# Latent attention of a hybrid backbone: two places for a pair's keys, three or four for its queries, keys split from PSUM, queries copied whole and rotated in SBUF

## The chip, the cores and the metric

One core of one Trainium2 chip runs the whole program in one launch. The metric is the device time of one execution in microseconds (us). A time is the median of several runs of the same program; one further execution was taken by the hardware profiler, and all rows shown here come from that one.

## The reference, cut to what matters

Two layers run over 256 latent tokens (the x stream) and 256 context tokens. Each layer mixes tokens in three ways (A windowed grouped-query attention, B multi-head latent attention, C gated linear attention), merges the three branches by gates, and ends with a gated convolutional feed-forward network. The second layer has no context output. The change touches branch B alone:

```
q  = (rmsnorm(cq)  @ w_uq ).reshape(.., 8 heads, 64 + 32)   # 64 plain, 32 rotary columns a head
kv = (rmsnorm(ckv) @ w_ukv).reshape(.., 8 heads, 64 + 64)   # 64 key columns, 64 value columns a head
q_rot = rope(q[.., 64:])        # latent tokens only; context queries stay as they are
k_rot = rope(bkr)               # one rotary key of 32 columns, shared by all 8 heads
s = (q_plain . k_plain + q_rot . k_rot) * 96 ** -0.5
out = softmax(s) @ v            # latent queries read context and latent keys, context queries context keys
```

## The kernel before, in words

Tokens lie along the free axis: a tile of 128 partitions and 512 columns holds 128 features of 256 latent and 256 context tokens. In layer 0 a query tile has W = 512 columns (NS = 2 streams), in layer 1 only the 256 latent ones (NS = 1). Every fp32 product is made of three matmuls on pieces of reduced precision: `mm3` multiplies hi by hi, hi by lo and lo by hi. A tile is cut into these pieces by `split(src, hi, lo)`: ScalarE (ACT) casts src to hi, VectorE (DVE) writes src - hi to lo. In the trace these are lines L188 and L189; for weights they are L164 (ACT) and L168 (DVE or GpSimd, POOL), both in `load_w`.

`attn_run` runs branch A and then branch B, each over four pairs of heads, with the score steps (pair, stream, half of the queries): 16 steps a branch in layer 0, 8 in layer 1. In a step, `scores` issues the matmuls of L818 into the PSUM tile `s`, takes the row maximum (L824), the exponentials (L834) and scales them (L840). `step_on` then does one part of what the next pair needs, and `values` of the step before transposes its probabilities (L856) and splits them (`pth` on L860, `ptl` on L861). Between the steps stand the fills: units of the merge of another branch (a gate of eight k-tiles or a product of four), which keep TensorE (PE) busy; L783, L787 and L789 read their PSUM. `outputs` (L872, L875) multiplies the probabilities with the values once both halves of a stream are there.

For branch B the next pair's parts are, from `prep_b(pr)`, in this order: `keys`, `vals`, `queries(0)`, `queries(1)`; then `ready()` is called behind the scores of the pair's last step and hands over the operands of the next pair's scores. In layer 0 one part goes with each of four steps, in layer 1 all go within two.

- `keys` multiplies into a PSUM tile `kp` and copies its two halves of 64 rows to SBUF (`kf`, L936).
- `queries(hh)` multiplies into a PSUM tile `qp`, whose rows are 64 plain columns, 32 rotary ones, and the same 32 again with the halves exchanged. ACT copies rows 0 to 63 to `qf` (L945), DVE forms the rotary rows with two products that read `qp` (L947, L948) and a sum (L949), and in layer 0 ACT copies the context half of the rotary rows (L951).
- `ready()` splits `kf` and `qf` of both heads. There is one place for a pair's keys, the tiles `kh` and `kl` (L420 to L424), which branch A's keys had before; the rotary rows 64 to 95 of it are split from `cgk` once, for the first pair. The queries have two places, the tag `q` (L426).

`kp`, `qp`, the values' tile and the fills all take turns on the PSUM tag `mm`, which has two banks. Each engine executes its queue in order. The order in the queues is laid down when the program is built: a planner goes through the instructions by their place in the source and by when it takes them to be ready.

Of the kernel before, what the change touches and what calls it, by code (L numbers as in the profile page):

```python
# [7 lines left out]
F32R = mybir.dt.float32r  # L8
# [3 lines left out]
ALU = mybir.AluOpType  # L12
# [6 lines left out]
T = 256  # L19
NTOK = 512  # L20
# [12 lines left out]
def hybrid(nc, tc, I, out, dbg=None, stop=None):  # L33
# [3 lines left out]
    V, S, G = nc.vector, nc.scalar, nc.gpsimd  # L37
# [5 lines left out]
    def pool(name, bufs=1):  # L43
        return tc.tile_pool(name=name, bufs=bufs, reuse_waits="tile")
# [5 lines left out]
    def psum(tag, w=512):  # L50
        return ps.tile([128, 512], F32, tag=tag, name="ps_" + tag, bufs=2)[:, :w]
# [11 lines left out]
    def wtile(name):  # L63
        return small.tile([128, 512], F32, tag="w", name=name, bufs=4)
# [4 lines left out]
    tabB = cst[:, C_TB:C_TB + 256]  # L69
# [101 lines left out]
    def mm3(o, ah, al, bh, bl, start, stop):  # L171
        mm(o, ah, bh, start=start, stop=False)  # L172
        mm(o, ah, bl, start=False, stop=False)  # L173
        mm(o, al, bh, start=False, stop=stop)  # L174
# [12 lines left out]
    def split(src, hi, lo, eng=None):  # L187
        S.copy(hi, src)  # L188
        (eng or V).tensor_tensor(out=lo, in0=src, in1=hi.bitcast(F32), op=ALU.subtract)  # L189
# [127 lines left out]
    def layer(l):  # L317
        last = l == L - 1
        lo_on_pool(0, 1)
        W = T if last else NTOK  # L320
        NS = W // T
# [3 lines left out]
        def inunit(t, w, p=None):  # L325
            return unit(win[l, t], Hh, Hl, w, p=p)
# [7 lines left out]
        with pool(f"mods{l}") as mp:  # L334
            if not last:
# [11 lines left out]
                                       in1=cs.rearrange("p (k s) -> p k s", s=2), op0=ALU.add, op1=ALU.mult)  # L347
# [32 lines left out]
            for streams in ([[0], [1]] if last else [[0, 1]]):  # L380
                c0, wd = T * streams[0], T * len(streams)
                for k in range(KT):
                    q = slice(c0, c0 + wd)
# [33 lines left out]
        cgk = yb_.tile([96, NTOK], F32, name="cgk")  # L417
        av_ = yb_.tile([128, 4, 2, 2, 64], F32R, name="av")

        def k_tile(n):  # L420
            return yb_.tile([128, 2, NTOK], F32R, tag="kh", name="kh")[:n]

        def l_tile(n):
            return yb_.tile([128, 2, NTOK], F32R, tag="kl", name="kl")[:n]  # L424

        def q_tile(n):  # L426
            return yb_.tile([128, 2, W], F32R, tag="q", name="q", bufs=2)[:n]
# [6 lines left out]
        with pool(f"c{l}") as cp:  # L434
# [17 lines left out]
            t1 = small.tile([128, 256], F32, tag="r1", name="t1", bufs=1)  # L452
# [87 lines left out]
            for t in range(2):  # L540
                gg = pair2("st"[t])
                for d in range(2):
                    g = gg[:, d]
# [10 lines left out]
            for t in range(2):  # L554
                for d in range(2):
                    g = mn[t][:, d]
# [93 lines left out]
            def rope_raw(t, w, scale):  # L650
                raw = wtile("araw")
                S.activation(raw[:, :w], inunit(t, w), AF.Copy, scale=scale)
                return raw
# [4 lines left out]
            for t in range(2):  # L658
                kx = cp.tile([128, 2 * NTOK], F32, tag="ex", name="kx", bufs=3).rearrange("p (a b) -> p a b", a=2)[:, :, :T]
# [9 lines left out]
            for t in range(2):  # L669
                kx = kxs[t]  # L670
# [65 lines left out]
            def rope(raw, bank="mm"):  # L736
                rp = psum(bank, T)
                mm(rp, perm, raw[:, :T], start=True, stop=True)
                t1 = small.tile([128, 256], F32, tag="r1", name="t1", bufs=1)
                V.tensor_tensor(out=t1, in0=rp, in1=sinA, op=ALU.mult)  # L740
                G.tensor_tensor(out=raw[:, :T], in0=raw[:, :T], in1=cosA, op=ALU.mult)
                V.tensor_tensor(out=raw[:, :T], in0=raw[:, :T], in1=t1, op=ALU.add)
# [56 lines left out]
        common = st2.enter_context(pool(f"att{l}"))  # L799
# [119 lines left out]
                    pv()  # L919
            return hd.get(4)  # L920

        kb, yb = [], []

        def prep_b(pr):
            if pr == 4:
                return [], None
            vb = common.tile([128, 4, 2, 2, 64], F32R, tag="vb", name="vb", bufs=2)
            kf, qfs, kv = [], [], []

            def keys():  # L930
                kv.extend(load_w(I["wukv"][l, pr], 256))
                kp = psum("mm")
                mm3(kp, kv[0][:, :128], kv[1][:, :128], ckh, ckl, True, True)
                for i in range(2):
                    kf.append(wtile("kf")[0:64])
                    S.copy(kf[i], kp[64 * i:64 * i + 64])  # L936

            def queries(hh):
                uqh, uql = load_w(I["wuq"][l, pr][:, 256 * hh:256 * hh + 256], 256)
                qp = psum("mm", W)  # L940
                for k in range(2):
                    c = slice(128 * k, 128 * k + 128)
                    mm3(qp, uqh[:, c], uql[:, c], cqh[k], cql[k], k == 0, k == 1)
                qf = wtile("qf")[:96, :W]
                S.copy(qf[0:64], qp[0:64])  # L945
                t1 = small.tile([128, 256], F32, tag="r1", name="t1", bufs=1)
                V.tensor_tensor(out=t1[64:96], in0=qp[64:96, :T], in1=tabB[64:96], op=ALU.mult)  # L947
                V.tensor_tensor(out=qf[64:96, :T], in0=qp[96:128, :T], in1=tabB[96:128], op=ALU.mult)  # L948
                V.tensor_tensor(out=qf[64:96, :T], in0=qf[64:96, :T], in1=t1[64:96], op=ALU.add)  # L949
                if NS == 2:  # L950
                    S.copy(qf[64:96, T:], qp[64:96, T:])  # L951
                qfs.append(qf)

            def vals():
                p = psum("mm")
                for tt in range(4):
                    c = slice(128 * tt, 128 * tt + 128)
                    mm3(p[:, c], ckh[:, c], ckl[:, c], kv[0][:, 128:256], kv[1][:, 128:256], True, True)
                split(p.rearrange("p (a h d) -> p a h d", a=4, h=2), vb[:, :, :, 0], vb[:, :, :, 1])

            def ready():
                if pr == 0:
                    kb.extend([k_tile(96), l_tile(96)])
                    for i in range(2):
                        split(cgk[64:96], kb[0][64:96, i], kb[1][64:96, i])
                qq = []
                for i in range(2):
                    split(kf[i], kb[0][0:64, i], kb[1][0:64, i])
                    qb = q_tile(96)
                    qh, ql = qb[:, 0], qb[:, 1]  # L970
                    split(qfs[i], qh, ql)
                    qq.append([(qh, kb[0][:, i]), (qh, kb[1][:, i]), (ql, kb[0][:, i])])
                return qq, vb, lambda: (yb[0][pr], yb[1][pr])
            return [keys, vals, lambda: queries(0), lambda: queries(1)], ready

        def prep_a(j):
            if j == 4:
                return prep_b(0)
            q, qt = [], [] if j else [q2]
            parts = [] if j == 0 else [lambda: q.append(rope_raw(T_AQ + j, W, 0.125)), lambda: rope(q[0])]  # L980

            def ready():
                if j:
                    qt.append(q_tile(128))
                    q_halves(q[0], qt[0])
                return [[(qt[0][:, i], k2[:, i]), (qt[0][R[i], i], kl[R[i]])] for i in range(2)], av_, lambda: (yah(j), yal[j])
            return parts, ready
# [58 lines left out]
        with pool(f"f{l}") as fp, ExitStack() as rst:  # L1046
# [3 lines left out]
            for s in range(NS):  # L1050
                q = slice(T * s, T * s + T)
# [244 lines left out]
```

## Time and profile before

| what | value |
|---|---|
| median of 3 runs | 1510.85 us (1507.99 to 1511.19) |
| the profiled execution | 1507.28 us, of which the span from the first to the last instruction is 1505.1 us |
| PE, share of the span in matmuls | 95% |
| DVE busy | 81% |
| ACT busy | 54% |
| POOL busy | 31% |
| granted TensorE clock, mean | 0.99 |
| branch B's score steps | about 330 to 446 us (layer 0) and 1155 to 1240 us (layer 1) |

A row of the timeline gives the start in us, the duration, the engine, the line, the operation, what it writes and reads, and in brackets how long its engine was idle before it and what ended that. A row of waits gives who waited for whom, the total in us, the number of times and the longest. A matmul row lasts longer than it holds the engine: matmuls overlap, and their ends are modelled, so the time that PE loses is read from its idle time.

### The profile page before, as it was taken

To read this page: it belongs to the slowest core of one execution; us is meant where nothing else is said; L and a number is where in the kernel's file an instruction comes from. 1 tells how busy PE (TensorE), PEld (TensorE's weight loads), DVE (VectorE), ACT (ScalarE), POOL (GpSimd) and SP (SyncE) were. 2 spreads that over 40 slices of the span, in tenths; PEclk is the share of its full clock that TensorE was granted. 3 is DMA by queue.
4 is the path that set the end of the run, shared out by engine and by line. 5 is a ranking of instruction groups with operands and counts; after the bars stand their busy time and mean duration, and the time that the engine had idled before them with its cause. 6 is when DMAs were issued, how large, how long until landed. Compare 5 with 4: busy or idle time off the path is not lost. (4 is left out here: it accounts for less than half of the span.)

```text
span 1505.1 us, 27723 instructions
## 1 busy us (share of the span) xinstructions
PE 1432.6 (95%) x10062; PEld 1238.0 (82%) x10062; DVE 1221.2 (81%) x2292; ACT 809.7 (54%) x1696; POOL 460.3 (31%) x351
## 2 busy tenths in 40 slices
PE   7989989999999999999999999999899899989997
PEld 4767867777788899788888888978788889989997
DVE  4699597788897779798877979989787876997885
ACT  3565345566664346533244235676467766665663
POOL 0023233232230000545644550004354343133331
PEclk9999999999999999999999999999999999999999
DMA  8512123232235565454644875543232336656553
GB/s 306 173 42 82 43 81 95 88 92 84 88 106 176 167 209 184 134 168 134 237 133 135 253 278 160 155 133 114 64 102 85 99 108 183 176 165 196 173 173 95
DMA packets 108584, 213.28 MB, mean 142 GB/s; under 512 B 12128, under 2 KB 21728, under 8 KB 107424
## 3 DMA queue, kind: packets, MB, share of 16 engines
q1 hardware_dynamic: 107760, 210.86, 45.0%
q8 instruction: 79, 1.29, 0.4%
q10 hardware_dynamic: 688, 0.66, 0.1%
q14 instruction: 57, 0.47, 0.1%
HBM read 210.42 MB, written 1.05 MB: 141 GB/s over the span
## 5 line engine op out<-in xcount | busy, mean ns | idle before, releaser
L168 POOL TENSOR_TENSOR wlo<-raw,whi 128x512 fp32r<-128x512 f32 (+1 forms) x270 | 374.5, 1392 | 717.1 <-ACT whi L164 518.2
L164 ACT CAST whi<-raw 128x512 fp32r<-128x512 f32 (+1 forms) x614 | 360.4, 598 | 310.8 <-PE ps_mm L173 129.0
L172 PE MATMUL ps_mm<-hh,whi 128*128 128x512 f32 (+1 forms) x808 | 296.1, 366 | 3.3 <-DVE qf L948 2.0
L174 PE MATMUL ps_mm<-hh,wlo 128*128 128x512 f32 (+1 forms) x808 | 291.4, 361 | 1.6 <-DVE wlo L168 1.6
L173 PE MATMUL ps_mm<-hl,whi 128*128 128x512 f32 (+1 forms) x808 | 291.6, 361 | 0.0
L168 DVE TENSOR_TENSOR wlo<-raw,whi 128x512 fp32r<-128x512 f32 (+1 forms) x344 | 236.0, 696 | 39.1 <-ACT whi L164 36.8
L172 PEld LDWEIGHTS ps_mm<-hh,whi 128*128 128x128 f32 x808 | 154.3, 191 | 29.8 <-issue 3.2
L174 PEld LDWEIGHTS ps_mm<-hh,wlo 128*128 128x128 f32 x808 | 154.0, 191 | 26.9 <-DVE wlo L168 2.0
L173 PEld LDWEIGHTS ps_mm<-hl,whi 128*128 128x128 f32 x808 | 154.4, 191 | 23.6 <-issue 0.4
L104 DVE SCALAR_TENSOR_TENSOR jk<-wm,sil 128x1024 f32<-128x1024 f32 x96 | 153.2, 1596 | 2.8 <-DMA wm<-wmod 1.9
L172 PE MATMUL ps_pair<-hh,whi 128*128 128x512 f32 (+1 forms) x312 | 110.5, 355 | 1.3 <-DVE cy L1094 1.0
L174 PE MATMUL ps_pair<-hh,wlo 128*128 128x512 f32 (+1 forms) x312 | 109.6, 354 | 0.5 <-DVE wlo L168 0.5
L173 PE MATMUL ps_pair<-hl,whi 128*128 128x512 f32 (+1 forms) x312 | 109.8, 352 | 0.0
L860 ACT CAST pth<-ps_pair 128x512 fp32r<-128x512 f32 (+1 forms) x96 | 49.4, 515 | 43.9 <-PE ps_pair L856 25.8
L606 POOL TENSOR_TENSOR ex<-ex,qk 128x512 f32<-128x512 f32 (+1 forms) x28 | 36.4, 1308 | 113.4 <-ACT ex L600 90.6
L172 PEld LDWEIGHTS ps_pair<-hh,whi 128*128 128x128 f32 x312 | 59.1, 190 | 11.2 <-ACT whi L164 2.6
L174 PEld LDWEIGHTS ps_pair<-hh,wlo 128*128 128x128 f32 x312 | 58.7, 189 | 10.0 <-DVE wlo L168 1.1
L173 PEld LDWEIGHTS ps_pair<-hl,whi 128*128 128x128 f32 x312 | 59.1, 189 | 8.8
L861 DVE TENSOR_TENSOR ptl<-ps_pair,pth 128x512 fp32r<-128x512 f32 (+1 forms) x96 | 57.3, 597 | 10.6 <-ACT pth L860 9.9
L172 PE MATMUL ps_mm<-ach,whi 128*128 128x256 f32 (+1 forms) x200 | 63.7, 319 | 1.0 <-ACT ach L1127 0.7
L173 PE MATMUL ps_mm<-acl,whi 128*128 128x256 f32 (+1 forms) x200 | 63.5, 317 | 0.0
L174 PE MATMUL ps_mm<-ach,wlo 128*128 128x256 f32 (+1 forms) x200 | 63.4, 317 | 0.0
(674 smaller groups left out, 3582.9 us busy)
## 6 DMA issues: line engine op xcount, KB each, us to landing
raw<-wup SPq DMA_DIRECT2D x184, 256.0 KB, 3.2
raw<-win SPq DMA_DIRECT2D x182, 256.0 KB, 2.7
wm<-wmod SPq DMA_DIRECT2D x64, 512.0 KB, 4.2
raw<-wdn SPq DMA_DIRECT2D x88, 256.0 KB, 3.0
raw<-wbr SPq DMA_DIRECT2D x48, 256.0 KB, 2.7
raw<-wout SPq DMA_DIRECT2D x48, 256.0 KB, 3.1
wm<-wm SPq DMA_DIRECT2D x8, 1024.0 KB, 6.6
wm<-wmod SPq DMA_DIRECT2D x32, 256.0 KB, 2.6
```

The source lines that it names most:

```text
L104: V.scalar_tensor_tensor(out=jk, in0=wm, scalar=1.0, in1=sil[:, s], op0=ALU.mult, op1=ALU.mult, accum_out=MOD[l][:, s, t:t + 1])
L164: S.copy(hi[:, :ncols], raw[:, :ncols])
L168: e.tensor_tensor(out=lo[:, :ncols], in0=raw[:, :ncols], in1=hi[:, :ncols].bitcast(F32), op=ALU.subtract)
L172: mm(o, ah, bh, start=start, stop=False)
L173: mm(o, ah, bl, start=False, stop=False)
L174: mm(o, al, bh, start=False, stop=stop)
L606: e.tensor_tensor(out=ex[:, i], in0=ex[:, i], in1=qk[t][:, i, :W], op=ALU.mult)
L860: S.copy(dh, tv)
L861: V.tensor_tensor(out=dl, in0=tv, in1=dh.bitcast(F32), op=ALU.subtract)
```

## The change

`kbuf(pr)` gives the keys two places: even pairs use two new tiles of the pool `common`, odd pairs the old `kh` and `kl`. Each place gets its rotary rows split from `cgk` when it is first asked for: the even place in branch A, as a third part of the preparation of A's pair 3, the odd place in `keys` of B's pair 1. `keys` splits the two halves of `kp` from PSUM straight into the place; `kf` is gone. `queries` copies all 128 rows of `qp` to `qf` and makes both rotary products from SBUF; the copy of L951 is gone. The queries have three places in layer 0 (NXQ = 1) and four in layer 1 (NXQ = 2): a head below NXQ is split in its `queries` part, the other one in `ready()`.

```
+        def kbuf(pr):
+            b = pr % 2
+            if b not in kb:
+                kb[b] = [k_tile(96), l_tile(96)] if b else [common.tile([128, 2, NTOK], F32R, name="kx" + g)[:96] for g in "hl"]
+                for i in range(2):
+                    split(cgk[64:96], kb[b][0][64:96, i], kb[b][1][64:96, i])
+            return kb[b]
+        def qbuf():
+            n = nq[0] % (NXQ + 2)
+            nq[0] += 1
+            return common.tile([128, 2, W], F32R, tag="qx", name="qx", bufs=NXQ)[:96] if n < NXQ else q_tile(96)
+        NXQ = (1, 2)[l]
...
+                b = kbuf(pr)
                 for i in range(2):
-                    kf.append(wtile("kf")[0:64])
-                    S.copy(kf[i], kp[64 * i:64 * i + 64])
+                    split(kp[64 * i:64 * i + 64], b[0][0:64, i], b[1][0:64, i])
...
-                qf = wtile("qf")[:96, :W]
-                S.copy(qf[0:64], qp[0:64])
+                qf = wtile("qf")[:, :W]
+                S.copy(qf, qp)
                 t1 = small.tile([128, 256], F32, tag="r1", name="t1", bufs=1)
-                V.tensor_tensor(out=t1[64:96], in0=qp[64:96, :T], in1=tabB[64:96], op=ALU.mult)
-                V.tensor_tensor(out=qf[64:96, :T], in0=qp[96:128, :T], in1=tabB[96:128], op=ALU.mult)
+                V.tensor_tensor(out=t1[64:96], in0=qf[64:96, :T], in1=tabB[64:96], op=ALU.mult)
+                V.tensor_tensor(out=qf[64:96, :T], in0=qf[96:128, :T], in1=tabB[96:128], op=ALU.mult)
                 V.tensor_tensor(out=qf[64:96, :T], in0=qf[64:96, :T], in1=t1[64:96], op=ALU.add)
-                if NS == 2:
-                    S.copy(qf[64:96, T:], qp[64:96, T:])
-                qfs.append(qf)
+                qfs.append(qf[:96])
+                if hh < NXQ:
+                    pair_q(hh)
+            def pair_q(hh):
+                qbs.append(qbuf())
+                split(qfs[hh], qbs[hh][:, 0], qbs[hh][:, 1])
...
             def ready():
-                if pr == 0:
-                    kb.extend([k_tile(96), l_tile(96)])
-                    for i in range(2):
-                        split(cgk[64:96], kb[0][64:96, i], kb[1][64:96, i])
-                qq = []
-                for i in range(2):
-                    split(kf[i], kb[0][0:64, i], kb[1][0:64, i])
-                    qb = q_tile(96)
-                    qh, ql = qb[:, 0], qb[:, 1]
-                    split(qfs[i], qh, ql)
-                    qq.append([(qh, kb[0][:, i]), (qh, kb[1][:, i]), (ql, kb[0][:, i])])
+                for hh in range(NXQ, 2):
+                    pair_q(hh)
+                hi, lo = kbuf(pr)
+                qq = [[(q[:, 0], hi[:, i]), (q[:, 0], lo[:, i]), (q[:, 1], hi[:, i])] for i, q in enumerate(qbs)]
...
+            if j == 3:
+                parts.append(lambda: kbuf(0))
```

## Rows read from the trace of the kernel before

**Rows 1.** Windows of branch B, both layers: us, busy (x) of PE, PEld, DVE, ACT, POOL.
```profile
322.00:446.00 124.00, 117.39 (x626) 97.03 (x625) 106.92 (x220) 78.58 (x185) 37.88 (x32) 1.00 0.31 92
1148.00:1240.00 92.00, 83.55 (x632) 76.99 (x632) 77.05 (x143) 65.07 (x152) 40.33 (x29) 1.00 0.33 101
```
**Rows 2.** Waits of PE, layer 0, 300 to 446 us: total, times, longest.
```profile
PE ps_pair L856 <- DVE ptl L861: 3.9, 2, 2.5
PE ps_pair L818 <- ACT q L188: 1.9, 2, 1.1
```
**Rows 3.** Waits of PE, layer 1, 1136 to 1240 us.
```profile
PE ps_mm L172 <- DVE qf L948: 3.1, 5, 1.2
...
PE ps_mm L172 <- ACT whi L164: 1.2, 1, 1.2
PE ps_mm L172 <- DVE m L787: 0.7, 1, 0.7
PE ps_pair L818 <- DVE q L189: 0.4, 1, 0.4
```
**Rows 4.** Timeline of DVE, the key splits at layer 0's change from A to B.
```profile
330.41 2.44 DVE L189 TENSOR_TENSOR kl<-kf,kh 64x512 fp32r<-64x512 f32 x2
```
**Rows 5.** Timeline of DVE just before PE's matmul of 1196.35 us.
```profile
1195.78 0.43 DVE L948 TENSOR_TENSOR qf<-ps_mm,cst 32x256 f32<-32x256 f32 x1
```
**Rows 6.** Tile kf, the copies: duration ns min/median/max, first and last start.
```profile
L936 ACT COPY kf<-ps_mm x16: 578/582/587, 302.3 to 1202.1; 64x512 f32<-64x512 f32 x16
```
**Rows 7.** Tile qf, the rotary sums and the context copy of layer 0.
```profile
L949 DVE TENSOR_TENSOR qf<-qf,t x16: 417/418/1399, 321.7 to 1216.8; 32x256 f32<-32x256 f32 x16
...
L951 ACT COPY qf<-ps_mm x8: 362/363/364, 321.0 to 432.3; 32x256 f32<-32x256 f32 x8
```
**Rows 8.** Groups of DVE, 320 to 1220 us: busy us, mean ns, then idle before.
```profile
L189 DVE TENSOR_TENSOR kl<-kf,kh 64x512 fp32r<-64x512 f32 x16 | 12.3, 773 | 0.3
...
L949 DVE TENSOR_TENSOR qf<-qf,t 32x256 f32<-32x256 f32 x16 | 11.0, 689 | 0.5
...
L948 DVE TENSOR_TENSOR qf<-ps_mm,cst 32x256 f32<-32x256 f32 x16 | 6.9, 429 | 0.2
L947 DVE TENSOR_TENSOR t<-ps_mm,cst 32x256 f32<-32x256 f32 x16 | 6.8, 422 | 0.7 <-ACT qf L945 0.4
...
L189 DVE TENSOR_TENSOR kl<-cgk,kh 32x512 fp32r<-32x512 f32 x4 | 3.1, 779 | 0.1
```
**Rows 9.** Tile vb, its split from PSUM.
```profile
L188 ACT CAST vb<-ps_mm x8: 583/586/587, 310.0 to 1209.0; 128x512 fp32r<-128x512 f32 x8
L189 DVE TENSOR_TENSOR vb<-ps_mm,vb x8: 671/689/693, 312.0 to 1209.6; 128x512 fp32r<-128x512 f32 x8
```
**Rows 10.** Waits of ACT, layer 0, 300 to 446 us.
```profile
ACT pth L860 <- DVE ptl L861: 9.4, 9, 2.8
...
ACT qf L951 <- DVE qf L948: 6.3, 5, 2.0
```
**Rows 11.** Windows of 8 us behind the keys' matmuls, columns as in Rows 1.
```profile
302.30:310.30 8.00, 7.84 (x51) 6.35 (x50) 7.08 (x17) 5.85 (x14) 0.95 (x1) 1.00 0.34 99
...
370.50:378.50 8.00, 6.89 (x32) 5.58 (x32) 7.53 (x16) 4.44 (x11) 0.86 (x2) 1.00 0.25 75
405.10:413.10 8.00, 6.73 (x43) 5.60 (x43) 7.93 (x18) 5.76 (x13) 1.28 (x1) 1.00 0.30 92
...
1201.40:1209.40 8.00, 7.10 (x54) 6.42 (x52) 5.80 (x11) 5.67 (x13) 2.90 (x2) 1.00 0.37 108
```
**Rows 12.** Timeline of PE, layer 0: the keys' last matmul, the values' first.
```profile
404.72 0.40 PE L174 MATMUL ps_mm<-ckh,wlo 128*128 128x512 f32 x1
...
406.45 0.22 PE L172 MATMUL ps_mm<-whi,ckh 128*128 128x128 f32 x1
```
**Rows 13.** Timeline, layer 1: a rotary sum beside a weight split on POOL.
```profile
1174.94 1.48 POOL L168 TENSOR_TENSOR wlo<-raw,whi 128x512 fp32r<-128x512 f32 x1
1175.30 1.40 DVE L949 TENSOR_TENSOR qf<-qf,t 32x256 f32<-32x256 f32 x1
```

More of the change, by code (lines that the diff above doesn't have):

```diff
@@ L920, in attn_run @@
             return hd.get(4)
-        kb, yb = [], []
+        kb, yb = {}, []
+        nq = [0]
+        def kbuf(pr):
[10 more added lines that the diff above has]
+        NXQ = (1, 2)[l]
         def prep_b(pr):
@@ L927, in prep_b @@
             vb = common.tile([128, 4, 2, 2, 64], F32R, tag="vb", name="vb", bufs=2)
-            kf, qfs, kv = [], [], []
+            qfs, qbs, kv = [], [], []
             def keys():
```

## The prediction

> **What bounds the kernel now.** I first read the busy time by stage. In branch B of layer 0 PE has matmuls for 117.39 of 124 us, in layer 1 for 83.55 of 92, and DVE is the next engine with 106.92 and 77.05 [rows 1]. So PE sets the pace, and the change can win only idle time of PE: 6.6 us in layer 0 (124 - 117.39), 8.4 us in layer 1. Next I read PE's waits in both stretches, widened to branch A's last pair, where the preparation of B begins. The reader is to see two kinds. In layer 0 PE waits 3.9 us for probability splits on DVE (`ptl`) and 1.9 us for the cast of queries that the next scores read [rows 2]. In layer 1 the largest is 3.1 us, in five places, where a matmul wants a bank of the tag `mm` that the rotary product L948 has still to read [rows 3]. Then I followed single waits back in the timeline. The longest of layer 0 (2.5 us) stands behind a burst on DVE: at the change of pair two key splits take 2.44 us in one go, and the `ptl` that PE wants comes behind them [rows 4]. The 1.2 us put down to a weight cast [rows 3] are a bank wait too: L948 ends at 1195.78 + 0.43 = 1196.21 us [rows 5], PE goes on at 1196.35.
>
> **What goes: the bank of a query projection.** Today `qp` is read by ACT, twice by DVE, and in layer 0 by ACT once more; afterwards by one ACT copy. That copy is 128x512 or 128x256 from PSUM; the nearest row is the cast of the values, 0.586 us for 128x512 [rows 9], so it takes what the 64-row copy takes now. L948 no longer stands between PE and the bank, and ACT's blocked time behind it (6.3 us in layer 0 [rows 10]) goes with L951 itself (8 x 0.363 us [rows 7]). I count the 3.1 and 1.2 us [rows 3] as gone: **4.3 us**. Next in line for that bank is ACT's copy alone, some 1 us earlier. If ACT is late with it, half comes back: bounds 2.2 to 4.3.
>
> **What goes: the burst at the change of pair.** `ready()` now splits four tiles behind the last scores. Afterwards it splits one (layer 0) or none (layer 1), and it no longer waits until the old pair's scores have left the only key tiles. With the burst gone I count as gone the longest wait for `ptl` (2.5), the wait for the cast of queries (1.9) [rows 2], the wait for their low part (0.4), and half of the 0.7 us for L787, which queues in the same burst [rows 3]: 2.5 + 1.9 + 0.4 + 0.3 = **5.1 us**. The other `ptl` wait of layer 0, 1.4 us, is at the middle of a pair and I leave it. Of the 1.9 us, head 1's cast stays on the path (its projection still comes in the last step); two key splits and one query split less stand before it on DVE, about 2 us, which is more than the longest of these waits (1.1). Bounds 2.5 to 5.1.
>
> The `kf` copies (16 x 0.582 us [rows 6]) were on ACT, in idle time; I count them at nothing. In all ACT loses 12.2 us of copies and gains four casts of about 0.6 [rows 9]. Nothing that moves issues a DMA, and the weight loads keep their order, so SP's queue is as before.
>
> **What comes: key splits in the `keys` step.** Eight times (four pairs, two layers) two DVE subtractions move from `ready()` to just behind the keys' matmuls, ahead of the `ptl` of the step before. They read PSUM; the nearest row is the values' split, 0.689 us [rows 9], against 0.773 now [rows 8], so DVE's own sum falls by 1.3 us and the load to be placed is 8 x 1.38 = 11.0 us. DVE's idle time in the 8 us behind each keys' step covers it or not: 8 - 7.08 = 0.92, 0.47 and 0.07 us at three places of layer 0; 2.20 at the least idle of the other five [rows 11]. Uncovered are 0.46, 0.91 and 1.31. The last two follow a burst that is now shorter, so I take half of them (1.1); and 1.0 in all for layer 1, where idle time may lie on the wrong side of a `ptl`. **2.6 us**, bounds 0 and 11.0.
>
> **The key bank.** A PSUM tile read by two engines is read in turns: ACT's second `pth` cast waited 9.4 us in nine places for DVE's first `ptl` [rows 10]. So `kp` will go cast, subtract, cast, subtract: 2 x (0.58 + 0.69) = 2.5 us against 1.16 for the two copies. The values' matmuls want the bank 406.45 - (404.72 + 0.40) = 1.3 us after the keys at the tightest place [rows 12]. Queued behind the waiting second cast are the exponentials on ACT and behind these the scaling on DVE. PE has other units to issue meanwhile; I take **0.5 us**, bounds 0 and 2 (twice 1.2 us, at two tight places, less rounding).
>
> **The second place.** Two more halves of `cgk` are split in each layer: 4 x 0.6 on ACT and 4 x 0.78 = 3.1 us on DVE [rows 8], and the first place's splits move from A's end into A's pair 2. I take 0.7 for the place in layer 0's branch A and 0.4 for the odd place: **1.1 us**, bounds 0 and 3.1.
>
> **The rotation from SBUF.** L947 and L948 have one input in PSUM and take 422 and 429 ns on average. L949 has both in SBUF and takes 689 ns on average [rows 8], 417 at its quickest and 1399 at its slowest [rows 7]: at 1175.30 us it lasts 1.40 and ends 0.28 us after a POOL split that had started before it [rows 13]. The 32 products now join that kind: at the mean they cost 32 x 0.689 - 13.7 = 8.3 us more of DVE, less the 1.3 of the key splits, which leave it: 7.0. At L949's quickest they cost nothing. A run of three shares one blocking, so I expect the delay to move from the sum to the first product rather than to triple: **0.4 us** on the path. [...]
>
> **Sum.** Gone 4.3 + 5.1 = 9.4; new 2.6 + 0.5 + 1.1 + 0.4 = 4.6; net -4.8 us. The profiled execution took 1507.28 us and would take 1502.5. It lies 3.6 us under the median of 1510.85, against which I predict: **1506.0 us**. A measurement of this kernel can tell 0.2%, 3.0 us, from no change.
>
> **Rivals.**
> 1. *The new work is hidden everywhere.* All idle time found holds it: -9.4, 1501.4 us. For it: five of eight places have 2.2 us or more [rows 11]. Against it: layer 0's DVE is 86% busy (106.92 / 124 [rows 1]).
> 2. *The burst only changes its place.* The bank waits go (-4.3), but the 5.1 us come back as waits for `ptl` in the `keys` step: -4.3 + 4.6 = +0.3, 1511.1 us. For it: DVE loses almost nothing in sum, and most of PE's waits end on DVE.
> 3. *The keys' chain in PSUM decides, and the kernel is slower.* Each `keys` step holds DVE for 1.38 us ahead of `ptl` and ACT behind it, and no idle time takes it: 11.0 + 3.1 + 0.5 + 0.4 = 15.0, less 9.4: +5.6, 1516.4 us. It decides from about 0.9 us a step on ((9.4 - 2.0) / 8). For it: two steps of layer 0 with hardly any idle DVE. Against it: the five others.
> 4. *DVE and POOL collide at the rotation.* 7.0 us in place of 0.4: +1.8, 1512.7 us. For it: the excess of today's sums, 16 x (689 - 418) ns = 4.3 us, is that of four or five long ones, and they could become three times as many. Against it: half of the sums take no more than 418 ns [rows 7].
>
> **How the numbers follow.** Forecast 0.49, rival 1 0.16, rival 2 0.18, rival 3 0.12, rival 4 0.05. The forecast's own bounds are about 1502 to 1510; some 0.41 of its 0.49 lies below 1507.8. Faster: 0.41 + 0.16 + 0.01 = 0.58. Same: 0.07 + 0.16 + 0.04 = 0.27. Slower: 0.01 + 0.01 + 0.12 + 0.01 = 0.15. The range must take in rivals 1, 2 and 4 and the near side of 3: 1500 to 1514.
>
> **What would show it.** Bank waits: PE has no wait for L948, and none of its kind for the copy. Burst: PE's waits for `q` and the 2.5 us for `ptl` at layer 0's change from A to B are gone; one key split stands no more in the DVE queue there. Keys: subtractions of 0.69 us from `ps_mm` behind each keys' matmul, PE's waits for `ptl` in `outputs` grown by about 2.6 us. Rotation: products of more than 0.45 us beside POOL. ACT: about 10 us less busy. I am wrong if waits for `ptl` or `pth` in branch B grow by more than 7 us, if PE waits on `kp`'s bank before the values, or if stages that the change does not touch move.

## The result: slower by 0.75%

| | before | after |
|---|---|---|
| median, us | 1511.02 (1507.99 to 1511.50) | 1519.76 (1517.71 to 1520.92) |
| ratio | | 1.0075, 95% interval 1.0056 to 1.0095 |
| profiled execution, span, us | 1507.28, 1505.1 | 1517.71, 1515.9 |
| mean granted clock of TensorE | 0.990 | 0.986 |

Forecast were 1506.0 us, faster, in a range of 1500 to 1514 us. The measured time is slower and lies above the range.

I laid the two traces over each other by the order of PE's matmuls and read how much later the same matmul comes. From branch B of layer 0 up to branch B of layer 1 the kernel after is ahead by 0.5 to 4.3 us (1.7 us are won in branch B of layer 0). In layer 1's branch B it loses 10.3 us, and 1.0 us more behind it. The windows of the two branches, between the same matmuls as in [rows 1] (us, then busy (x) of PE, PEld, DVE, ACT and POOL, granted clock, DMA share, GB/s):

```profile
321.50:443.80 122.30, 117.21 (x626) 97.30 (x625) 106.50 (x219) 72.19 (x169) 39.22 (x33) 1.00 0.32 98
1147.10:1249.40 102.30, 88.61 (x632) 81.24 (x631) 82.44 (x142) 61.05 (x144) 39.60 (x29) 0.95 0.29 90
```

Layer 1: 92.0 us have become 102.3. PE's idle time rose from 8.45 to 102.30 - 88.61 = 13.69 us (+5.2). The other half is the granted clock, the first column behind the busy times: it was 1.00 and is 0.95, and 0.05 x 102.3 = 5.1 us. By as much PE is busy longer with the same 632 matmuls (88.61 - 83.55). Together 10.3. DVE is busy 5.4 us longer, ACT 4 us less.

PE's waits in layer 1 from 1134 to 1250 us, the answer to [rows 3]:

```profile
PE ps_pair L818 <- ACT q L188: 3.0, 2, 2.6
PE ps_pair L856 <- DVE p L840: 2.7, 1, 2.7
PE ps_pair L818 <- DVE q L189: 2.6, 2, 1.5
PE ps_o L875 <- DVE ptl L861: 2.4, 3, 1.1
...
PE ps_mm L172 <- ACT qf L962: 0.5, 1, 0.5
```

The bank waits (3.1 us for L948, 1.2 put down to a weight cast) are gone, as forecast; ACT's copy L962 left 0.5. In their place the scores (L818) wait 3.0 + 2.6 us for the split of the queries, where it was 0.4 before, and the transposes (L856) wait 2.7 us for the scaled probabilities `p`. In layer 0 (298 to 444 us) the answer to [rows 2] is:

```profile
PE ps_o L875 <- DVE ptl L861: 2.3, 4, 0.9
PE ps_pair L856 <- DVE ptl L861: 1.7, 2, 1.5
PE ps_pair L818 <- ACT qx L188: 0.6, 1, 0.6
PE ps_pair L818 <- ACT q L188: 0.6, 1, 0.6
```

The single 2.5 us is gone, but waits for `ptl` are still 4.0 us in all, in six places. Before they were 4.4 us in four, for beside the 3.9 of [rows 2] stood:

```profile
PE ps_o L875 <- DVE ptl L861: 0.5, 2, 0.3
```

Windows of 10 us show where the clock went in layer 1:

```profile
1150.00:1160.00 10.00, 6.78 (x44) 6.40 (x43) 9.16 (x18) 4.89 (x14) 3.91 (x3) 0.83 0.27 81
1180.00:1190.00 10.00, 8.53 (x44) 7.08 (x44) 8.10 (x16) 5.62 (x14) 2.76 (x3) 0.83 0.22 54
1220.00:1230.00 10.00, 5.89 (x35) 4.82 (x34) 9.72 (x15) 3.68 (x8) 4.41 (x3) 0.89 0.46 144
1230.00:1240.00 10.00, 10.00 (x76) 9.66 (x75) 6.77 (x14) 6.06 (x15) 3.11 (x2) 0.94 0.25 77
```

0.17 x 10, 0.17 x 10 and 0.11 x 10 + 0.06 x 10 are three losses of 1.7 us, each behind idle time of PE: 2.66 us up to 1156.4 (for `p`), 1.06 + 0.41 + 0.43 us about 1181 (for `q`, `gt`, `q`), 2.60 and 1.51 us up to 1228.1 (for `q`). In the kernel before, every window of 10 us between 1100 and 1320 us stood at 1.00. Not every such wait is followed by the lower clock: before, the 2.5 us up to 334.9 us were not (layer 0's window in [rows 1] is at 1.00), and after, 2.1 us up to 1007.3 us were not. So the clock's half of the loss is what one execution shows, and the table of the experiments gives it apart from idle time.

The last of these places shows the mechanism. Timeline after, the change to pair 3 in layer 1 (start us, us; a bracket is idle time and what ended it):

```profile
1217.59 1.29 POOL L168 TENSOR_TENSOR wlo<-raw,whi 128x512 fp32r<-128x512 f32 x1 [5.27 <-ACT whi L164]
1217.81 1.34 DVE L964 TENSOR_TENSOR t<-qf,cst 32x256 f32<-32x256 f32 x1
1219.19 0.69 DVE L168 TENSOR_TENSOR wlo<-raw,whi 128x512 fp32r<-128x512 f32 x1
1219.91 0.42 DVE L965 TENSOR_TENSOR qf<-qf,cst 32x256 f32<-32x256 f32 x1
...
1221.84 0.42 DVE L964 TENSOR_TENSOR t<-qf,cst 32x256 f32<-32x256 f32 x1
...
1222.60 1.27 POOL L168 TENSOR_TENSOR wlo<-raw,whi 128x512 fp32r<-128x512 f32 x1 [0.19 <-PE ps_mm L174]
1222.74 1.42 DVE L965 TENSOR_TENSOR qf<-qf,cst 32x256 f32<-32x256 f32 x1
1224.19 0.69 DVE L861 TENSOR_TENSOR ptl<-ps_pair,pth 128x512 fp32r<-128x512 f32 x1
1224.91 0.42 DVE L966 TENSOR_TENSOR qf<-qf,t 32x256 f32<-32x256 f32 x1
...
1225.88 0.50 PE L818 MATMUL ps_pair<-kh,q 96*128 96x512 f32 x1 [2.60 <-ACT q L188]
...
1228.11 0.80 PE L818 MATMUL ps_pair<-kh,q 96*128 96x512 f32 x1 [1.51 <-DVE q L189]
```

Two of the six products and sums last 1.34 and 1.42 us instead of 0.42, each from just behind the start of a POOL split until 0.28 us behind its end. And other work stands between the links of the rotation: L965 overwrites the rows that L964 reads, and the order that comes out of the build puts a weight split or a `ptl` between them. So head 1's queries are rotated 7.5 us after head 0's rotation began (before it took 6.2 us, 1212.03 to 1218.24), and PE has nothing else to do. The first of the three places is another case: there PE waits for `p`, and e11 below, with POOL's work left out, still waits 1.8 us for the same matmul and loses the clock behind it. What delays that place is not shown.

### The profile page after: what moved, and what is told of

Same layout as the page of the kernel before. It is cut to its first block, busy times and chain, and to the rows that moved or that the text cites. A ratio compares the mean times of both kernels' runs of the same rounds, so it can differ in the third digit from the quotient of the medians.

```text
span 1515.9 us, 27707 instructions
## 1 busy us (share of the span) xinstructions
PE 1437.1 (95%) x10062; PEld 1240.5 (82%) x10062; DVE 1229.8 (81%) x2296; ACT 802.9 (53%) x1676; POOL 463.2 (31%) x351
## 5 line engine op out<-in xcount | busy, mean ns | idle before, releaser
L104 DVE SCALAR_TENSOR_TENSOR jk<-wm,sil 128x1024 f32<-128x1024 f32 x96 | 149.9, 1562 | 1.7 <-DMA wm<-wmod 0.7
L861 DVE TENSOR_TENSOR ptl<-ps_pair,pth 128x512 fp32r<-128x512 f32 (+1 forms) x96 | 57.3, 597 | 12.2 <-ACT pth L860 11.2
```

Source lines behind the costliest of these rows:

```text
L104: V.scalar_tensor_tensor(out=jk, in0=wm, scalar=1.0, in1=sil[:, s], op0=ALU.mult, op1=ALU.mult, accum_out=MOD[l][:, s, t:t + 1])
L861: V.tensor_tensor(out=dl, in0=tv, in1=dh.bitcast(F32), op=ALU.subtract)
```

## The experiments

Each trace was laid over that of before in the same way. The columns "layer 0" and "layer 1" say how many us the matmuls of before between 322 and 446 (branch B of layer 0) and between 1148 and 1250 us (layer 1) took longer, in one profiled execution. The last column is for the same stretch of layer 1: PE's idle time, then what the lower clock cost (1 minus the granted clock, times the stretch). The kernel after, e4, e6 and e9 share layer 0's code and give -1.7, -1.7, -1.7 and -1.6 there. Before, e4 and e17 share layer 1's code: their idle time is 8.5, 8.5 and 8.3 us, but the clock cost 0, 1.7 and 0. So idle time repeats, and 1.7 us in a layer's column can be the clock of one execution.

| run | rotation reads | else | ratio (95%) | layer 0 | layer 1 | layer 1: idle, clock |
|---|---|---|---|---|---|---|
| before | PSUM | | 1 | 0 | 0 | 8.5, 0 |
| after | SBUF | | 1.0075 (1.0056 to 1.0095) | -1.7 | +10.3 | 13.7, 5.1 |
| e1 | PSUM, as before | places of keys, queries | 1.0020 (1.0002 to 1.0038) | -3.8 | +4.3 | 9.6, 1.7 |
| e2 | SBUF | keys as before | 1.0124 (1.0095 to 1.0152) | +8.1 | +9.5 | 13.8, 5.1 |
| e3 | SBUF | queries as before | 1.0101 (1.0077 to 1.0125) | +2.6 | +10.2 | 14.2, 5.1 |
| e4 | SBUF in layer 0 | layer 1 as before | 0.9999 (0.9985 to 1.0012) | -1.7 | +1.7 | 8.5, 1.7 |
| e5 | SBUF | all else as before | 1.0131 (1.0108 to 1.0153) | +12.7 | +9.9 | 13.9, 5.1 |
| e6 | SBUF, PSUM in layer 1 | | 1.0022 (1.0005 to 1.0038) | -1.7 | +4.3 | 9.6, 1.7 |
| e7 | PSUM, behind whole copy | | 1.0011 (0.9996 to 1.0026) | -3.7 | +2.8 | 8.8, 1.7 |
| e8 | SBUF, copied by DVE | | 1.0130 (1.0107 to 1.0152) | +7.7 | +8.0 | 14.8, 0 |
| e9 | SBUF, own place | | 1.0050 (1.0034 to 1.0066) | -1.6 | +10.5 | 12.2, 8.5 |
| e10 | SBUF, bank held | | 1.0121 (1.0100 to 1.0143) | -0.1 | +11.8 | 15.9, 5.1 |
| e13 | SBUF | shared key split late | 1.0086 (1.0067 to 1.0105) | -1.8 | +9.3 | 12.7, 5.1 |
| e14 | as e7 | shared key split late | 1.0013 (0.9999 to 1.0026) | -4.5 | +1.5 | 8.4, 0 |
| e17 | PSUM, as before | places in layer 0 alone | 0.9984 (0.9970 to 0.9998) | -2.5 | 0.0 | 8.3, 0 |
| e18 | as e7 | places in layer 0 alone | 0.9979 (0.9964 to 0.9993) | -3.8 | -1.5 | 6.7, 0 |

The four runs with POOL changed (e11, e12, e15, e16) follow below.

### Which part of the change loses? (e1 to e6)

e1 takes the rotation back to PSUM in the changed kernel:
```
-                qf = wtile("qf")[:, :W]
-                S.copy(qf, qp)
+                qf = wtile("qf")[:96, :W]
+                S.copy(qf[0:64], qp[0:64])
...
-    V.tensor_tensor(out=t1[64:96], in0=qf[64:96, :T], ...)
+    V.tensor_tensor(out=t1[64:96], in0=qp[64:96, :T], ...)
```


> The changed kernel with the rotation as before (ACT copies rows 0 to 63, both rotary products read PSUM, L951's copy is back in layer 0); key places, key splits and query places stay changed. Theory R (the whole copy delays the rotation: the products wait for ACT, stand late in DVE's queue and collide with POOL, so head 1's cast is late for the next pair's scores in layer 1): the waits of PE for the query cast and low part in layer 1, 5.6 us, go, and with them two of the three stretches at half clock; 1508 to 1513 us. Theory K (key splits from PSUM hold DVE and ACT) and theory Q (early query splits): 1517 to 1522 us.

Measured 1510.42 us, ratio 1.0020. Theory R holds: most of the loss is gone, and of the three stretches at the lower clock one is left.

e2 takes back the keys (`kf` copies by ACT, one pair of places, splits in `ready()`):
```
-                b = kbuf(pr)
-                for i in range(2):
-                    split(kp[64 * i:64 * i + 64], b[0][0:64, i], ...)
+                for i in range(2):
+                    kf.append(wtile("kf")[0:64])
+                    S.copy(kf[i], kp[64 * i:64 * i + 64])
```


> The changed kernel with one place for the keys, kf copies and key splits in ready() as before; the whole copy, the rotation from SBUF and the three or four query places stay. Theory K: 1508 to 1513 us, waits behind the keys' matmuls gone. Theory R: still 1517 us or more, as the burst at the change of pair is back too: up to 1525 us.

Measured 1527.00 us, 7 us more than the changed kernel and 2 us more than theory R allowed; the +8.1 of layer 0 is where they are. Theory K is wrong with its sign: beside the rotation from SBUF, the early key splits help.

e3 takes back the early query splits (`NXQ = (0, 0)[l]`).

> The changed kernel with NXQ = (0, 0): two places for queries, both heads split in ready(); keys and rotation stay changed. Theory Q (a head that is split early lets the planner put the next scores earlier in PE's queue, where they then wait for head 1): 1508 to 1513 us, the waits of 2.6 and 1.5 us at layer 1's third change of pair gone. Theory R: 1516 to 1522 us, since the rotation is as late as before.

Measured 1522.94 us, ratio 1.0101, 0.9 us above theory R's answer: theory Q falls too.

e4 changes layer 0 alone (`if (1, 0)[l]` about both parts, `NXQ = (1, 0)[l]`).

> The change in layer 0 alone (keys, whole copy, three query places); layer 1 as before. All theories that put the loss into layer 1's branch B expect the loss to be gone: layer 0's own shift in the two profiles is -1 to -2 us, so 1508 to 1511 us. If the time stays above 1515 us, the loss is not tied to layer 1's edit but to where stages fall.

Measured 1508.63 us, ratio 0.9999: the loss comes with layer 1's code.

e5 is the kernel before with the new rotation alone:
```
-                qf = wtile("qf")[:96, :W]
-                S.copy(qf[0:64], qp[0:64])
+                qf = wtile("qf")[:, :W]
+                S.copy(qf, qp)
...  both products from qf instead of qp
```


> The kernel before with one part of the change alone: the query projection copied whole by ACT and rotated in SBUF, in both layers. One pair of key places, key copies on ACT and all splits in ready() as before. Theory R (the rotation alone makes the loss): slower than before by as much as the changed kernel, about +9 us or more, since nothing of the other parts' gain is there: ratio 1.006 to 1.011, with half-clock stretches in layer 1's branch B. Theory J (only together: the keys and queries that are ready earlier let PE run on to the rotation's chain): within 3 us of before, ratio 0.998 to 1.002.

Measured 1528.53 us, ratio 1.0131: 20 us by itself, where the whole change loses 11, so theory J falls. In this kernel layer 0 loses as well (136.7 us for 124, clock 0.94):

```profile
322.10:458.80 136.70, 124.93 (x626) 103.22 (x625) 111.96 (x221) 75.97 (x177) 37.00 (x33) 0.94 0.27 83
```

The largest wait of PE there, in layer 0 and layer 1, is for the cast of the queries:

```profile
PE ps_pair L818 <- ACT q L188: 6.5, 3, 3.1
...
PE ps_pair L818 <- ACT q L188: 6.3, 3, 2.6
```

So the places for keys and queries repair, in layer 0, what the rotation breaks; in layer 1 they don't.

e6 is the changed kernel with layer 1's rotation from PSUM (`if (1, 0)[l]` about the two forms).

> The changed kernel with layer 1's rotation read from PSUM again; layer 0 keeps the rotation in SBUF, all else stays changed. Theory R in its narrow form (the loss of the changed kernel lies in layer 1's rotation): the +9 us are gone, 1508 to 1512 us, ratio 0.999 to 1.003. If it stays above 1.005, layer 0's rotation or a shift that it causes carries a part.

Measured 1510.83 us, ratio 1.0022: as theory R says, the loss of the changed kernel lies in layer 1's rotation.

### Why does the rotation from SBUF lose? (e7 to e10)

e7 keeps the whole copy and the chain behind it, and reads the products from PSUM:
```
-    V.tensor_tensor(out=t1[64:96], in0=qf[64:96, :T], in1=tabB[64:96], op=ALU.mult)
-    V.tensor_tensor(out=qf[64:96, :T], in0=qf[96:128, :T], in1=tabB[96:128], op=ALU.mult)
+    V.tensor_tensor(out=qf[64:96, :T], in0=qp[96:128, :T], in1=tabB[96:128], op=ALU.mult)
+    V.tensor_tensor(out=t1[64:96], in0=qp[64:96, :T], in1=tabB[64:96], op=ALU.mult)
```


> The changed kernel, with the two rotary products reading the projection in PSUM but standing behind ACT's whole copy (the second product writes rows that the copy writes before, and is issued first). So the chain copy, products, sum is that of the changed kernel, no product has two inputs in SBUF, and the bank is held to the last product as before. Theory W (the chain waits for ACT's copy, which stands behind exponentials and casts): stays slow, 1516 to 1522 us, ratio 1.005 to 1.010. Theory C (products with two SBUF inputs wait for POOL): 1508 to 1512 us, ratio up to 1.003; no product over 0.5 us.

Measured 1508.35 us, ratio 1.0011. Waiting for ACT's copy (theory W) is not the cause. The same change of pair in this trace:

```profile
1214.13 0.43 DVE L964 TENSOR_TENSOR qf<-ps_mm,cst 32x256 f32<-32x256 f32 x1
1214.57 0.42 DVE L965 TENSOR_TENSOR t<-ps_mm,cst 32x256 f32<-32x256 f32 x1
1215.02 0.43 DVE L964 TENSOR_TENSOR qf<-ps_mm,cst 32x256 f32<-32x256 f32 x1
1215.48 0.42 DVE L966 TENSOR_TENSOR qf<-qf,t 32x256 f32<-32x256 f32 x1
...
1216.73 0.42 DVE L965 TENSOR_TENSOR t<-ps_mm,cst 32x256 f32<-32x256 f32 x1
...
1218.12 0.42 DVE L966 TENSOR_TENSOR qf<-qf,t 32x256 f32<-32x256 f32 x1
...
1219.61 0.40 PE L818 MATMUL ps_pair<-kl,q 96*128 96x512 f32 x1
```

From the first product to head 1's sum it takes 1218.54 - 1214.13 = 4.4 us instead of 7.5, no product is long, and PE goes through the scores without a wait. A pair of rows shows the products' source alone. At the first rotation of the branch the product starts 0.23 us behind the start of a POOL split in both kernels; after:

```profile
1146.27 1.29 POOL L168 TENSOR_TENSOR wlo<-raw,whi 128x512 fp32r<-128x512 f32 x1 [2.96 <-ACT whi L164]
1146.50 1.34 DVE L964 TENSOR_TENSOR t<-qf,cst 32x256 f32<-32x256 f32 x1 [0.39 <-ACT qf L962]
```

and in e7:

```profile
1145.57 1.29 POOL L168 TENSOR_TENSOR wlo<-raw,whi 128x512 fp32r<-128x512 f32 x1 [2.92 <-ACT whi L164]
1145.80 0.43 DVE L964 TENSOR_TENSOR qf<-ps_mm,cst 32x256 f32<-32x256 f32 x1 [0.39 <-ACT qf L962]
```

The rotary groups of DVE in layer 1's branch B, after (busy us, mean ns, idle before):

```profile
L964 DVE TENSOR_TENSOR t<-qf,cst 32x256 f32<-32x256 f32 x8 | 6.0, 747 | 0.7 <-ACT qf L962 0.4
L965 DVE TENSOR_TENSOR qf<-qf,cst 32x256 f32<-32x256 f32 x8 | 4.5, 558 | 0.3
L966 DVE TENSOR_TENSOR qf<-qf,t 32x256 f32<-32x256 f32 x8 | 3.3, 417 | 0.3
```

and in e7:

```profile
L964 DVE TENSOR_TENSOR qf<-ps_mm,cst 32x256 f32<-32x256 f32 x8 | 3.4, 428 | 0.6 <-ACT qf L962 0.4
L965 DVE TENSOR_TENSOR t<-ps_mm,cst 32x256 f32<-32x256 f32 x8 | 3.4, 422 | 0.2
L966 DVE TENSOR_TENSOR qf<-qf,t 32x256 f32<-32x256 f32 x8 | 3.3, 417 | 0.2
```

13.8 us against 10.1: all of the difference is in the two products.

e8 lets DVE copy the rows that it rotates:
```
-                S.copy(qf, qp)
+                V.tensor_copy(out=qf[64:128], in_=qp[64:128])
+                S.copy(qf[0:64], qp[0:64])
```


> The changed kernel, with rows 64 to 127 of the query projection copied by DVE itself just ahead of the products, and only rows 0 to 63 by ACT as before. The products still read SBUF twice (POOL can hold them up), the bank is free after the two copies, and nothing of the rotation waits for ACT. DVE gets 16 copies more, some 0.4 to 0.7 us each, about 9 us of its own sum. Theory W: the loss goes in the most part, 1509 to 1514 us, ratio up to 1.004. Theory C: no gain and the copies on top, 1519 to 1525 us, ratio 1.007 to 1.012.

Measured 1527.66 us, ratio 1.0130: nothing of the rotation waits for ACT, and the loss is larger. Theory W falls a second time; theory C expected less than this.

e9 gives the second product a place of its own in layer 1:
```
+    t2 = qw[64:96, T:] if NS == 1 else qf[64:96, :T]
-    V.tensor_tensor(out=qf[64:96, :T], in0=qf[96:128, :T], ...)
-    V.tensor_tensor(out=qf[64:96, :T], in0=qf[64:96, :T], in1=t1[64:96], op=ALU.add)
+    V.tensor_tensor(out=t2, in0=qf[96:128, :T], ...)
+    V.tensor_tensor(out=qf[64:96, :T], in0=t2, in1=t1[64:96], op=ALU.add)
```


> The changed kernel; in layer 1 the second rotary product goes to a place of its own (columns 256 to 511 of the same tile, unused there) instead of overwriting the rows that the first product reads. The two products no longer depend on each other, so other work of DVE need not stand between them; they still read SBUF twice, the bank is still freed by ACT's copy. Theory D (in place, the three instructions of the rotation are a chain, and DVE's queue has other work between its links): the most part of the loss goes, 1509 to 1514 us, ratio up to 1.004. Theories C (products held up by POOL) and B (the bank freed early sends PE on to scores that aren't ready): stays at 1517 to 1521 us, ratio 1.005 to 1.009.

Measured 1514.28 us, ratio 1.0050, just above theory D's answer and below the other; its interval overlaps that of the changed kernel. Its traced execution took longer than its median (1519.29 us): the clock cost 8.5 us in layer 1 there, while PE's idle time fell from 13.7 to 12.2 us. Products beside a POOL split are as long as before (up to 1.41 us). So the chain in place is a part of the cause, and not the main part of the idle time.

e10 holds the bank:
```
+    V.tensor_copy(out=qf[96:128, 0:4], in_=qp[96:128, 0:4])   # behind the sum
```


> The changed kernel with a copy of 32x4 elements from the projection's bank behind the second product, on DVE (16 of them, an estimate of 0.16 us each from the smallest DVE rows, 2.6 us in all): the bank is held to that point, as with a rotation from PSUM, while the products still read SBUF. Theory B: the loss goes, 1508 to 1513 us. Theories C and D: no gain, 1518 to 1524 us, ratio 1.006 to 1.011.

The copy stands behind the sum, one instruction later than the second product, so the bank is held somewhat longer than was meant. Measured 1523.93 us, ratio 1.0121. PE now waits for the bank (layer 1), and the loss is greater; theory B falls:

```profile
PE ps_mm L172 <- DVE qf L967: 9.1, 4, 2.9
```

### Is it POOL? (e11, e12, e15, e16)

e11 and e12 leave out POOL's instructions in branch B:
```
+        if skip[0] and lo_mix[2] % lo_mix[1] < lo_mix[0]:
+            lo_mix[2] += 1
+            return hi, hi
...
-                for i in range(2):
+                for i in range(skip[0] and (0, 1)[l], 2):
```


> The changed kernel without POOL's work in branch B of both layers: the low parts of weights that POOL would compute are left out (the high part stands in their place) and so is POOL's scaling of probabilities in layer 1; both parts of the computation are missing from the output. To be read only beside the next run, which leaves out the same. Theory C: the rotation then costs nothing beside the next run, within 3 us of it. Theories B and D: 6 to 12 us above it.

> The same part of POOL's work left out (low parts of weights and the scaling that POOL has in branch B), with the rotation reading PSUM behind ACT's whole copy. The control for the run before: with POOL at work the two differ by some 11 us (1519.8 against 1508.4). Theory C: the difference falls under 3 us. Theories B and D: it stays at 6 to 12 us.

Measured 1501.93 us (ratio 0.9963, 0.9950 to 0.9976) and 1500.83 us (0.9956, 0.9939 to 0.9973). With POOL at work the two rotations are 0.0064 of 1508 = 9.7 us apart (changed kernel and e7, by the ratios), without it 1.1 us. e11 loses nothing in layer 1's branch B (-1.1). PE's idle time there says the same without the clock: 13.7 us after against 8.8 in e7, and 5.8 in e11 against 4.2 in e12.

But both are faster than before, so slack was gained too. e15 and e16 keep an instruction of POOL at each place, one that reads nothing:
```
+        if skip[0] and e is G:
+            G.memset(lo[:, :ncols].bitcast(F32), 0.0)
+            return hi, lo
...
+                if skip[0] and l:
+                    G.memset(pts[1], 0.0)
```


> The changed kernel; in branch B each of POOL's instructions (low parts of weights, and in layer 1 its scaling of probabilities) is replaced by a memset of the same tile: these parts of the computation are missing from the output. POOL then writes SBUF and reads nothing there. To be read beside the next run. Theory C (a POOL instruction that reads SBUF holds up DVE's products with two SBUF inputs): no rotary product over 0.5 us, and within 3 us of the next run. Rival L (POOL's instruction as such, its delay or its writing): 6 to 12 us above the next run.

> The control for the run before: POOL's instructions in branch B replaced by memsets in the same way (the same parts of the computation are missing), the rotation reading PSUM behind ACT's whole copy. Theory C: within 3 us of the run before. Rival L: 6 to 12 us below it.

Measured 1505.67 us (0.9983, 0.9968 to 0.9997) and 1502.58 us (0.9967, 0.9950 to 0.9984): 2.4 us apart by the ratios, with 6.4 and 5.1 us of idle time in layer 1. With the rotation from SBUF, the rotary instructions of e15 in layer 1 (ns min/median/max, first and last start):

```profile
L970 DVE TENSOR_TENSOR t<-qf,cst x8: 416/417/1336, 1146.2 to 1214.3; 32x256 f32<-32x256 f32 x8
L971 DVE TENSOR_TENSOR qf<-qf,cst x8: 420/420/421, 1148.8 to 1215.2; 32x256 f32<-32x256 f32 x8
L972 DVE TENSOR_TENSOR qf<-qf,t x8: 416/417/418, 1149.8 to 1216.4; 32x256 f32<-32x256 f32 x8
```

One of 24 is long, and it is the one that still meets a weight split on POOL, left from branch A:

```profile
1145.94 1.28 POOL L172 TENSOR_TENSOR wlo<-raw,whi 128x512 fp32r<-128x512 f32 x1 [2.94 <-ACT whi L165]
...
1146.17 1.34 DVE L970 TENSOR_TENSOR t<-qf,cst 32x256 f32<-32x256 f32 x1 [0.39 <-ACT qf L968]
```

So beside the weight split, which reads SBUF, the product took 1.34 us, and the other 23 took 0.42 us while POOL had 24 memsets in the branch, which only write it (16 of 0.51 and 8 of 0.53 us on average). Theory C holds for the weight split; how many of the 23 overlap a memset in time is not shown. What stays open is its share: the memsets are also shorter (0.5 us against 1.2 for a split), and part of the vanished loss may be the slack that this gives.

### Do the shared key splits cost? (e13, e14)

e1 and e7 lose about 3 us in layer 1's branch A, where a split of the shared key rows stands in DVE's queue long before it is needed. e13 (on the changed kernel) and e14 (on e7) issue it behind the keys' copies:
```
-            if j == 3:
-                parts.append(lambda: kbuf(0))
+                    with tc.issue_after(r.ins):      # r: the cast of the keys
+                        for i in range(2):
+                            split(cgk[64:96], b[0][64:96, i], b[1][64:96, i])
```


> The changed kernel, with the split of the shared key rows into a new pair of places held back until the keys of that pair have been copied (in the changed kernel the one of layer 1 stands in DVE's queue some 40 us earlier, at the start of branch A). Theory P (these early splits cost PE a wait of 1.9 us at the start of layer 1's branch A, with a half-clock stretch behind it, and stand in the full queue at the change from A to B): 3 to 6 us less than the changed kernel, 1514 to 1517 us, ratio 1.003 to 1.006; the rotation's loss stays. Rival (the splits are hidden): 1518 to 1521.

> The same holding back, with the rotation reading PSUM behind ACT's whole copy, which alone gave 1508.4 us. Theory P: 1503 to 1506 us, faster than before by some 3 us, ratio 0.997 to 0.999, no wait of PE over 1 us at the start of layer 1's branch A. Rival: 1507 to 1510 us.

Measured 1519.96 us (ratio 1.0086) and 1509.60 us (1.0013): no gain. In e14 PE still waits 1.9 us there, now for the exponential. So it does, eight matmuls before the place of e1 and e7, in e2, e4, e5, e17 and e18 (1.8 to 1.9 us), which have no such split in layer 1: theory P falls. The edit also has a price of its own, a wait of 1.5 us for the split of the held-back place (L953) up to 1137.5 us in e14, with 3.4 us of clock behind it. What costs the 3 us is open.

### What are the places worth by themselves? (e17, e18)

Both keep them in layer 0 alone (`if (1, 0)[l]` as in e4), with the rotation of before (e17) and of e7 (e18).

> The kernel before, with the new places of keys and queries and the keys split from PSUM in layer 0 alone; rotation from PSUM as before in both layers, layer 1 as before. If layer 0's gain is kept to the end (e1's trace stood 5.2 us ahead at 1085 us): 1502 to 1505 us, ratio 0.996 to 0.999. If an earlier start of layer 1 is given back whatever its code: 1506 to 1510 us, ratio 0.999 to 1.002.

> The same places in layer 0 alone, with the rotary products reading PSUM behind ACT's whole copy, in both layers. The same two answers as for the run before: 1502 to 1505 us if layer 0's gain is kept, 1506 to 1510 us if it is given back.

Measured 1505.33 us (ratio 0.9984) and 1504.58 us (0.9979, interval 0.9964 to 0.9993). Both are at the upper end of the first answer (e17 0.3 us above it, its ratio inside): layer 0's gain is kept, and e18 beats both kernels, by 3.2 us on before.

## Why the prediction was wrong, point by point

**The rotation from SBUF, 0.4 us: the step that failed.** e7 differs from the kernel after in the products' source, with the order and the held bank that follow from it, and is 9.7 us quicker; e5 has it alone and is 20 us slower than before. I had written that the delay would "move from the sum to the first product rather than triple". In DVE's time this is nearly so: the rotation went from 24.7 us [rows 8] to 27.6 in both layers. What was wrong is that a delay of DVE counts once and by its own length. It stands in the chain to head 1's queries, the last link that PE wants at a change of pair, and 0.9 and 1.0 us on two links, with other work between them, became 2.6 + 1.5 us of idle PE there, with 1.7 us of clock behind them. No term of the sum was for the clock, which had been 1.00 [rows 1]; in the traced execution it took 5.1 us, half of the loss.

The rotation is not the whole miss. The forecast was a ratio of 0.997 and the result 1.0075; e7, without the rotation's loss, stands at 1.0011. So some 6 of the 16 us between forecast and result are gains that did not come, in layer 1 above all: the bank and the burst below.

**The rivals.** Rival 4 (DVE and POOL collide at the rotation) named the place and got 0.05. Its price of 7.0 us was taken from DVE's busy time, and so it ended at 1512.7 us for 1519.8. For its small chance I had argued that half of the sums take no more than 418 ns; the median product after is also 418 to 422 ns. Ten of the 32 were long (0.53 to 1.42 us), each beside a weight split on POOL, and they did the harm; each ends 0.28 us behind the end of its split. In layer 1 of e15 one product of 16 meets a weight split and takes 1.34 us; the others, with memsets for POOL's work, take 0.42. Beside POOL's scaling of probabilities (L840, 1.78 us) it was not so: two products of the kernel after that start 1.2 us into one, at 1178.29 and 1221.84 us, take 0.42.

**The bank, 4.3 us.** The waits went as forecast, and won nothing in layer 1. I read them as cover: while PE waited for the bank, head 1's chain ran; no run shows this by itself. e7 has 1.5 us of bank waits (for L965) and no wait of over 1 us for queries.

**The burst, 5.1 us.** "About 2 us less" before head 1's cast on DVE was the wrong sign in layer 1: head 1's rotation and split came later, not earlier. In layer 0 the longest wait went, the sum of waits for `ptl` only fell from 4.4 to 4.0 us, and that for the queries' cast from 1.9 to 1.2. The early places did win in layer 0: 3.8 us with the rotation from PSUM (e1), and with that from SBUF they turn the +12.7 of e5 into -1.7; of the whole time e18 keeps 3.2 us. In layer 1 e1, e7 and e14 are 1.5 to 4.3 us behind; in e1 and e7 1.7 us of it are the clock, and PE's idle time is 9.6, 8.8 and 8.4 us against 8.5. So they win nothing there; whether they lose is not settled.

**Keys in the `keys` step, 2.6 us, and rival 3.** The splits take 0.69 us as forecast, in layer 0:

```profile
L189 DVE TENSOR_TENSOR kxl<-ps_mm,kxh 64x512 fp32r<-64x512 f32 x4 | 2.7, 686 | 0.2
```

Rival 3 was to make the kernel slower by this chain; e2 takes it away, and is slower still.

**The key bank, 0.5, and the second place, 1.1 us.** PE has no wait for the keys' bank. ACT's waits between `pth` and `ptl` in layer 0 doubled (9.4 us in [rows 10]), and cost nothing that can be seen:

```profile
ACT pth L860 <- DVE ptl L861: 17.8, 13, 2.5
```

Holding the shared splits back (e13, e14) changed nothing measurable.

**What was to show me wrong.** I looked for waits for `ptl` and `pth` grown by 7 us. They didn't grow. The loss came through the wait that I had counted as gone. ACT is less busy by 6.8 us (809.7 to 802.9) where I said about 10.

## What to carry to other kernels

Before moving an operand from PSUM to SBUF to free a bank, look at what GpSimd runs at that moment (beside a weight split a product took up to 1.42 us here, for 0.42), and price the longest instance in the chain that the next matmul waits for, not the mean in the engine's sum. A bank wait that goes is a gain only if the next thing that PE wants is ready (here 4.3 us of bank waits went, and the scores' waits for the queries' split rose from 0.4 to 5.6 us); ask what ran under the wait. A new wait of about two microseconds on PE can cost more than its length: behind three of them here the clock cost 1.7 us each, behind others nothing.

## What the runs showed of the hardware

- In layer 1's branch B after, the granted clock fell three times from 1.00 to 0.50 of full speed behind about 2 to 4 us of idle time of PE, each time for a stretch that cost 1.7 us; in e7 it fell behind a wait of 1.9 us up to 1090.4 us (0.83 in the window 1090 to 1100, also 1.7 us). Other waits of that length had no such stretch behind them, the clock stayed at 1.00: 2.5 us up to 334.9 us before, 2.1 us up to 1007.3 us after; and e8, with 14.8 us of idle time in layer 1's branch B, stayed at 1.00 there. Executions differ in this with the same code (layer 1 of before and of e4: 0 and 1.7 us). The first of the three after, behind the wait up to 1156.4, as a window:

```profile
1156.50:1159.50 3.00, 3.00 (x15) 3.00 (x16) 2.75 (x5) 0.59 (x1) 1.04 (x2) 0.50 0.30 71
```

- A rotary product of 32x256 on DVE with two SBUF inputs took 0.42 us in 22 of 32 instances of the kernel after. The other ten, which start behind the start of a POOL weight split, took 0.53 to 1.42 us and end 0.28 us behind the split's end. In layer 1 of e15, with memsets (0.51 and 0.53 us) for POOL's work, 15 of 16 took 0.42.
- The same product with one input in PSUM took 0.42 to 0.43 us in all 32 instances of e7, with POOL at its usual work.
